# Where the first weight sums of the down projection stand in VectorE's order

## The chip, the cores and the metric

The kernel runs on one core of a Trainium2 chip. The metric is the device time of one execution in microseconds (us); for a set of runs it is their median. TensorE multiplies matrices, VectorE and ScalarE work on tiles, GpSimd does little here, and SyncE (SP) issues nearly all DMAs. Each engine works through its own instructions in one fixed order.

## The reference

A decoder trunk of two layers on 512 tokens of width 1024, in float32. Each layer is a half-step feed-forward block, a mixing block (three kinds of attention, gated and merged) and a second half-step feed-forward block. So there are four feed-forward blocks, named a0, c0, a1 and c1 here in their order in time. What matters is one of them:

```
def _swiglu(t, w_gate, w_up, w_down):
    return (jax.nn.silu(t @ w_gate) * (t @ w_up)) @ w_down

f = _swiglu(_rmsnorm(h, ffn1_pre_g[l]), ffn1_w_gate[l], ffn1_w_up[l], ffn1_w_down[l])
h = h + 0.5 * _rmsnorm(f, ffn1_post_g[l])
```

The hidden width is 2816, which is 22 tiles of 128.

## The kernel before

**Split operands.** A float32 product is made of three matmuls of a narrower format (mm3, lines 203 to 207): high times high, high times low, low times high. So each weight tile is split (lines 179 to 192): ScalarE casts the raw weight to its high part (wh, line 182), then VectorE subtracts that from the raw weight to get the low part (wl, line 183). Four buffers hold high parts and four hold low parts. A factor that comes from the hidden rows is split in the same way (ah, al).

**Seven products for eight.** Of the 22 hidden tiles, 16 are worked in two chunks of 8 (ci = 0, 1). In each chunk the hidden activations and the down weights are cut into 2 by 2 blocks, and the block product is made with seven products in place of eight, n = 0 to 6. Some products need sums of blocks. Line 282 says which weight block a product fetches; for n = 2 the sum is block (0, 1) minus block (0, 0). Block (0, 1) goes into a tile of its own that is kept for later products (bt, called bta and btc in the profile for the blocks a and c), block (0, 0) into a raw tile (raw_da, raw_dc), and line 327 subtracts one from the other on VectorE. Then the kept tile is split like any weight. Each product has two weight units of 128 x 1024 elements per tile, at k0 = 0 and k0 = 2; I call them a and b, and write (ci, n) for a product. The six hidden tiles that are left (f = 16 to 21) are worked plainly, and the gate and up products of the tiles 18 to 21 are put between the products of the down group.

**Order of the work.** products (lines 888 to 900) makes the down group's jobs in the order (0, 0), (1, 0), (0, 1), (1, 1), (0, 2), (1, 2), and so on (line 849). PLAN (lines 1643 to 1649) puts single jobs of the plain tiles between them. Around the change the order of the jobs is: (1, 0); gate of tile 18; (0, 1); (1, 1); gate of tile 19; (0, 2); up of tile 18; (1, 2); up of tile 19; (0, 3).

A queue (lines 350 to 461) works the jobs off. As a job begins, step calls load for its own weight units and then load_ahead, which loads the units of the following jobs until four units are counted. load (lines 318 to 331) fetches the unit if that has not been done, makes the sum where the product needs one, and splits. So the instructions of the loads are traced in this order:

- as the gate of tile 18 begins: the splits of (1, 1)a and (1, 1)b;
- as (0, 1) begins: sum and split of (0, 2)a, then sum and split of (0, 2)b;
- as (1, 1) begins: the splits of the up weights of tile 18, and behind them the factor of (0, 2) (first_factor, lines 829 to 847);
- as (0, 2) begins: sum and split of (1, 2)a, then of (1, 2)b.

**Order on the engine.** The order in which an engine gets its instructions is not the order of tracing. A scheduler sets it when the program is built, from priorities and from its own estimate of when each input is there. An instruction whose inputs it takes to be there early can thus go in front of others that were traced before it. tc.keep_in_program_order(ins) pins one instruction behind the one traced just before it on the same engine. That is an edge of order alone and adds no semaphore wait. In load the sum is pinned only while Q.pinned is set, which it is in one place (halved, lines 633 to 640, at the start of a block).

**Buffers and DMA.** Raw weights of the down group go into two rings: two buffers "raw" for the units a and two of the tag "o" for the units b. A raw buffer is free for the next transfer when its last reader is done; for (ci, 2) that is the sum, otherwise the low split. The up and gate weights of the plain tiles take "raw" buffers too. SyncE issues the transfers in its own fixed order.

Of the kernel before, what the change touches and what calls it, by code (L numbers as in the profile page):

```python
# [23 lines left out]
def kernel(  # L24
# [79 lines left out]
    def stile(shape, tag, name, dt=F32R):  # L104
        return sb.tile(shape, dt, tag=tag, bufs=BUFS[tag], name=name)
# [126 lines left out]
    class Unit:  # L232


        def __init__(self, src, k0, nk, c0, ncol, name, scale=None):
            self.tags, self.place = ("wh", "wl"), "raw"
            self.src, self.k0, self.nk, self.c0, self.ncol, self.name, self.scale = src, k0, nk, c0, ncol, name, scale
            self.h = self.raw = None
# [13 lines left out]
        def load(self):  # L252
            if self.h is not None:
                return
            self.fetch()
            self.split_from(self.raw[:])
            self.loaded()
# [16 lines left out]
    class BlockUnit(Unit):  # L274
# [9 lines left out]
        def __init__(self, n, src, rows, k0, nk, ncol, keep, name, place="raw"):  # L284
            super().__init__(src, k0, nk, 0, ncol, name)
            self.n, self.rows, self.keep, self.fetched, self.place = n, rows, keep, False, place
            self.heir = None

        def inherits(self, un):
            un.heir, self.place = self, None  # L290
# [27 lines left out]
        def load(self):  # L318
            if self.h is not None:
                return  # L320
            self.fetch()
            src = raw = self.raw[:]
            if self.n in (2, 3, 5, 6):
                t = self.keep.get(self.k0)
                src = raw if self.n == 5 else t
                a, b = (t, raw) if self.n in (2, 5) else (raw, t)
                ins = nc.vector.tensor_tensor(src, a, b, ALU.subtract)
                if Q.pinned:
                    tc.keep_in_program_order(ins)
            self.split_from(src)  # L330
            self.loaded()
# [131 lines left out]
    Q = Queue()  # L463
# [139 lines left out]
    def ffn(l, src, wg, wu, wd, dst, name, spare, parked, plan, aside=None):  # L603
# [247 lines left out]
        def product(at, uns):  # L851
            ci, n = DOWN[at]
            first, last = ci == 0, ci == NC - 1
            if at == 0:
                RINGS["o"] = 2
                dst.begin()
            if at + 1 < len(DOWN):
                first_factor(*DOWN[at + 1])
            if first and n in (0, 2):
                st["b", SUM[n]] = [pbank("z", f"pd{name}_{n}_{e}") for e in range(2)]  # L860
            pts = st["b", SUM[n]]
            h, l = st.pop(("a", ci, n))
            opens, ends = first and n in (0, 2), last and n in (1, 4, 6)
            for un in uns:
                for e in range(2):
                    c = slice(e * P, (e + 1) * P)
                    for k in range(un.nk):
                        kk = un.k0 + k
                        mm3(pts[e][:], h[:, kk, c], l[:, kk, c], un.h[:, k], un.l[:, k], opens and kk == 0,
                            ends and kk == FC // 2 - 1, free=True)  # L870
                        yield 3 * S * PE_US
                    turn(un.k0 + e)
            if not last:
                return
            if n == 0:
                st["b", 1] = [pbank("z", f"pd{name}_1_{e}") for e in range(2)]
                for e in range(2):
                    nc.scalar.copy(st["b", 1][e][:], pts[e][:])
                return
            i, hf = TO[n]  # L880
            for e in range(2):
                f = dst.fs[2 * i + e][:, HF[hf]]
                if n in (4, 5):
                    nc.vector.tensor_tensor(f, f, pts[e][:], ALU.add)
                else:
                    nc.scalar.copy(f, pts[e][:])

        def products():

            keep = [Keep(lambda k0, ci=ci: stile([P, 2, S], "o", f"bt{name}_{ci}_{k0}", F32)[:]) for ci in range(NC)]  # L890
            had = {}
            for at, (ci, n) in enumerate(DOWN):
                w = wd[l, ci * FC * P:(ci + 1) * FC * P]
                uns = [BlockUnit(n, w, FC // 2, k, 2, S, keep[ci], f"d{name}_{ci}_{n}_{k}", ("raw", "o")[k // 2])
                       for k in range(0, FC // 2, 2)]
                if n == 4:
                    for un, of in zip(uns, had[ci, 3]):
                        un.inherits(of)
                had[ci, n] = uns
                yield uns, (lambda at=at, uns=uns: product(at, uns))  # L900
# [18 lines left out]
        def queue(what):  # L919
            kind, n = what[0], what[1]  # L920
            if kind in "gu":
                if n not in made:
                    made[n] = plain(n)
                ms = (what[2],) if what[-1] in (0, 1) and len(what) == 3 else range(2)
                uns = made[n][kind == "u"]
                run = (lambda: gates(n, uns, ms)) if kind == "g" else (lambda: ups(n, uns, ms))
                Q.add(uns if ms[0] == 0 else [], run)
            elif kind == "a":
                Q.add([], lambda: iter(first_factor(n, 0) or ()))
            elif kind == "m":  # L930
                if name == "a0":
                    Q.add([], mem_stats)
            else:
                if what not in made:
                    made[what] = products() if kind == "d" else token_products(n, kind == "U")
                for one in made[what]:
                    Q.add(*one)
                    break
# [766 lines left out]
```

## Time and profile before

| | |
|---|---|
| median of three runs | 2383.31 us (2377.81 to 2385.16) |
| the profiled execution | 2377.93 us |
| its span, first to last instruction | 2376.2 us |
| mean granted clock of TensorE | 0.996 of full speed |
| VectorE busy | 1800.1 us, 76% of the span |
| ScalarE busy | 1511.8 us, 64% of the span |
| weight sums of product 2 in the down group (line 327) | 8 in blocks a, 1224 ns each, and 8 in blocks c, 1226 ns each (median) |

A timeline row of the profile gives the start and the length in us, the engine, the line of the kernel, the operation, the tile that is written and those that are read, and the shape. In brackets stand the idle time of the engine before it and what ended that time: "<-DMA raw_da" is a transfer into raw_da, "<-PE pda L207" a matmul of line 207 into pda. PE is TensorE, DVE is VectorE, ACT is ScalarE, SPq is SyncE's queue, where a row is the issue of a transfer and not the transfer. Buffers have no numbers, so two rows with the same tile names may be different units. In a list of waits a row reads: who waited, for whom, us in total, how often, the longest. PEclk is the clock that TensorE was granted, as a share of full speed.

### The profile page before, as it was taken

Reading aid. Unit: us, or ns where it says so; the run is one execution under the profiler, and the core shown is the slowest. Engines: PE = TensorE matmul, PEld = TensorE weight load, DVE = VectorE, ACT = ScalarE, POOL = GpSimd, SP = SyncE. Lnnn points to the kernel's source line nnn. Section 1 sums busy time; section 2 is a strip of 40 time slices with the busy share of each in tenths; the row PEclk is TensorE's granted clock in tenths of the full one; section 3 lists DMA queues with packets and bytes.
Section 4 is the critical chain, followed back from the end, with each engine's and each line's share of the span. In section 5 each row is a group of like instructions: output and inputs, shape, how many; then the busy total and the mean of one; then the engine's idle time right before and its main releaser. Section 6 shows DMA issues by size and latency. Waiting matters only on the chain.

```text
span 2376.2 us, 31130 instructions
## 1 busy us (share of the span) xinstructions
PE 2347.3 (99%) x11719; PEld 1986.0 (84%) x11719; DVE 1800.1 (76%) x2358; ACT 1511.8 (64%) x2305; POOL 75.4 (3%) x134
## 2 busy tenths in 40 slices
PE   9999999999999999999999999999999999999998
PEld 7787889888888888878888878899888888888787
DVE  8876877677777688868788768766767777887785
ACT  6776465576766556774556765646777665567744
POOL 0000000000111000000000000000000100000000
PEclk9999999999999999999999999999999999999999
DMA  5666454223323555664646664542323235566743
GB/s 204 185 177 199 154 190 142 80 83 88 89 74 104 192 189 160 186 186 146 226 127 198 205 171 147 194 129 72 94 76 98 72 117 188 174 185 175 214 144 142
DMA packets 299754, 354.98 MB, mean 149 GB/s; under 512 B 78266, under 2 KB 192978, under 8 KB 299604
## 3 DMA queue, kind: packets, MB, share of 16 engines
q1 hardware_dynamic: 299508, 352.97, 48.5%
q8 instruction: 92, 1.51, 0.3%
q14 instruction: 58, 0.48, 0.1%
q0 software_dynamic: 96, 0.03, 0.0%
HBM read 319.39 MB, written 16.78 MB: 141 GB/s over the span
## 4 chain that ended last, share of the span: by engine, by line
PE 89%; DMA 3%; DVE 3%; ACT 2%; issue 1%; SPq 0%; POOL 0%; DVEq 0%; ACTq 0%
PE pg L206 4%; PE pg L207 4%; PE pg L205 4%; PE pda L206 3%; PE pdc L206 3%; PE pda L207 3%; PE pda L205 3%; PE pdc L207 2%; PE pdc L205 2%; PE pb L206 2%; PE pb L207 2%; PE pb L205 2%; PE pwo L206 1%; PE pq L206 1%; PE pq L205 1%
## 5 line engine op out<-in xcount | busy, mean ns | idle before, releaser
L205 PE MATMUL pg<-us_a,wh_wg 128*128 128x512 f32 x384 | 151.0, 393 | 0.0
L206 PE MATMUL pg<-us_a,wh_wg 128*128 128x512 f32 x384 | 149.8, 390 | 0.0
L207 PE MATMUL pg<-us_a,wl_wg 128*128 128x512 f32 x384 | 149.8, 390 | 0.0
L206 PE MATMUL pda<-wl_da,aha 128*128 128x512 f32 x224 | 89.0, 398 | 6.6 <-DVE wl_da L183 6.6
L206 PE MATMUL pdc<-wl_dc,ahc 128*128 128x512 f32 x224 | 88.7, 396 | 6.1 <-DVE wl_dc L183 6.1
L183 DVE TENSOR_TENSOR wl_da<-raw_da,wh_da 128x1024 fp32r<-128x1024 f32 x50 | 60.8, 1223 | 37.4 <-ACT wh_da L182 37.3
L205 PE MATMUL pda<-wh_da,aha 128*128 128x512 f32 x224 | 88.2, 397 | 0.8 <-ACT wh_da L182 0.5
L207 PE MATMUL pda<-wh_da,ala 128*128 128x512 f32 x224 | 88.4, 395 | 0.0
L183 DVE TENSOR_TENSOR wl_dc<-raw_dc,wh_dc 128x1024 fp32r<-128x1024 f32 x50 | 60.9, 1222 | 35.8 <-ACT wh_dc L182 35.8
L207 PE MATMUL pdc<-wh_dc,alc 128*128 128x512 f32 x224 | 87.9, 393 | 0.0
L205 PE MATMUL pdc<-wh_dc,ahc 128*128 128x512 f32 x224 | 87.4, 393 | 0.4 <-ACT wh_dc L182 0.4
L207 PEld LDWEIGHTS pg<-us_a,wl_wg 128*128 128x128 f32 x384 | 72.1, 188 | 15.2
L205 PEld LDWEIGHTS pg<-us_a,wh_wg 128*128 128x128 f32 x384 | 72.1, 188 | 14.1
L206 PEld LDWEIGHTS pg<-us_a,wh_wg 128*128 128x128 f32 x384 | 72.2, 188 | 14.1
L182 ACT CAST wh_da<-raw_da 128x1024 fp32r<-128x1024 f32 x50 | 52.1, 1049 | 41.1 <-PE pda L207 11.1
L186 DVE SCALAR_TENSOR_TENSOR wl_wg<-raw_wg,wh_wg 128x1024 fp32r<-128x1024 f32 x48 | 58.4, 1221 | 23.0 <-ACT wh_wg L185 23.0
L182 ACT CAST wh_dc<-raw_dc 128x1024 fp32r<-128x1024 f32 x50 | 52.1, 1047 | 35.3 <-DMA raw_dc<-in_ffn_w_down_dram 11.5
L200 DVE SCALAR_TENSOR_TENSOR ga<-pg,bgate,ga 128x512 f32<-128x512 f32 x48 | 35.9, 747 | 48.7 <-ACT ga L199 48.7
L182 ACT CAST wh_uc<-raw_uc 128x1024 fp32r<-128x1024 f32 x44 | 46.4, 1054 | 37.6 <-PE pwc0g L207 8.6
L185 ACT ACTIVATE wh_wg<-raw_wg 128x1024 fp32r<-128x1024 f32 x48 | 50.5, 1057 | 25.5 <-PE pv L1096 11.7
L183 DVE TENSOR_TENSOR wl_uc<-raw_uc,wh_uc 128x1024 fp32r<-128x1024 f32 x44 | 53.7, 1220 | 16.7 <-ACT wh_uc L182 16.6
L182 ACT CAST wh_ua<-raw_ua 128x1024 fp32r<-128x1024 f32 x44 | 46.2, 1052 | 28.7 <-PE pga L206 7.2
(647 smaller groups left out, 8057.2 us busy)
## 6 DMA issues: line engine op xcount, KB each, us to landing
raw_da<-in_ffn_w_down_dram SPq DMA_DIRECT2D x66, 512.0 KB, 4.9
raw_dc<-in_ffn_w_down_dram SPq DMA_DIRECT2D x66, 512.0 KB, 3.8
raw_ga<-in_ffn_w_gate_dram SPq DMA_DIRECT2D x52, 512.0 KB, 4.7
raw_ua<-in_ffn_w_up_dram SPq DMA_DIRECT2D x52, 512.0 KB, 4.6
raw_gc<-in_ffn_w_gate_dram SPq DMA_DIRECT2D x52, 512.0 KB, 4.1
raw_uc<-in_ffn_w_up_dram SPq DMA_DIRECT2D x52, 512.0 KB, 4.2
raw_wg<-in_w_gate_dram SPq DMA_DIRECT2D x48, 512.0 KB, 3.5
raw_wo<-in_w_out_dram SPq DMA_DIRECT2D x24, 512.0 KB, 3.6
```

Of the source, the lines that this page charges most:

```text
L182: both = [nc.scalar.copy(h_ap, src)]
L183: make = lambda: nc.vector.tensor_tensor(l_ap, src, h_ap.bitcast(F32), ALU.subtract)
L185: both = [nc.scalar.activation(h_ap, src, AF.Copy, scale=scale)]
L186: make = lambda: nc.vector.scalar_tensor_tensor(l_ap, src, scale, h_ap.bitcast(F32), ALU.mult, ALU.subtract)
L200: nc.vector.scalar_tensor_tensor(t, z, minus, t, ALU.max, ALU.add)
L205: nc.tensor.matmul(pt, lh, rh, start=start, stop=False, skip_group_check=free)
L206: nc.tensor.matmul(pt, lh, rl, start=False, stop=False, skip_group_check=free)
L207: nc.tensor.matmul(pt, ll, rh, start=False, stop=stop, skip_group_check=free)
```

## The change

A weight unit gets a mark, behind. products sets it on the units of product 2, in both chunks and in all four feed-forward blocks. Where it is set, load pins the sum of line 327 behind the instruction traced just before it on VectorE, as Q.pinned does. Sums of the other products, and those of the gate and up groups (token_products), stay as they were.

```diff
@@ BlockUnit.__init__
-            self.heir = None
+            self.heir, self.behind = None, False
@@ BlockUnit.load
                 ins = nc.vector.tensor_tensor(src, a, b, ALU.subtract)
-                if Q.pinned:
+                if Q.pinned or self.behind:
                     tc.keep_in_program_order(ins)
@@ products
                 uns = [BlockUnit(n, w, FC // 2, k, 2, S, keep[ci], f"d{name}_{ci}_{n}_{k}", ("raw", "o")[k // 2])
                        for k in range(0, FC // 2, 2)]
+                for un in uns:
+                    un.behind = n == 2
                 if n == 4:
```

## The prediction

> **What bounds the kernel now.** I read the page first, then the waits of TensorE alone, then the timelines of VectorE, ScalarE, TensorE and the DMA queue around the longest of those waits, and last a table by stretch for the clock.
>
> ```profile
> span 2376.2 us, 31130 instructions
> ...
> PE 2347.3 (99%) x11719; PEld 1986.0 (84%) x11719; DVE 1800.1 (76%) x2358; ACT 1511.8 (64%) x2305; POOL 75.4 (3%) x134
> ```
>
> TensorE is busy in all but 28.9 us of its span. A change of order on VectorE can therefore pay in two ways only: it takes away part of those 28.9 us, or it takes away matmuls that run slowly. The waits of TensorE say who owns the idle time:
>
> ```profile
> PE pda L206 <- DVE wl_da L183: 6.6, 2, 4.3
> PE pdc L206 <- DVE wl_dc L183: 6.1, 2, 4.4
> ```
>
> Four waits, 12.7 us, all of the down group (pda, pdc) and all for the low part of a weight (wl). One lies in each of the four feed-forward blocks. I write (ci, n) for product n of chunk ci, and a and b for its two weight units. In the first block VectorE's timeline reads:
>
> ```profile
> 213.49 1.23 DVE L327 TENSOR_TENSOR bta<-bta,raw_da 128x1024 f32<-128x1024 f32 x1 [2.38 <-DMA raw_da<-in_ffn_w_down_dram]
> 216.17 1.22 DVE L327 TENSOR_TENSOR bta<-bta,raw_da 128x1024 f32<-128x1024 f32 x1 [1.46 <-DMA raw_da<-in_ffn_w_down_dram]
> 217.32 1.22 DVE L183 TENSOR_TENSOR wl_da<-raw_da,wh_da 128x1024 fp32r<-128x1024 f32 x1
> 218.45 1.22 DVE L183 TENSOR_TENSOR ala<-asa,aha 128x1024 fp32r<-128x1024 f32 x1
> 219.59 1.22 DVE L838 TENSOR_TENSOR asa<-hra,hra 128x1024 f32<-128x1024 f32 x1
> 220.72 1.22 DVE L183 TENSOR_TENSOR wl_da<-raw_da,wh_da 128x1024 fp32r<-128x1024 f32 x1
> ```
>
> The first two rows are the weight sums of (0, 2), units a and b. Both sit waiting for their DMA. Behind them, with no idle time of their own, come the low parts of (1, 1)a at 217.32 and (1, 1)b at 220.72, a product that runs *earlier*. ScalarE and TensorE beside it:
>
> ```profile
> 214.12 1.04 ACT L182 CAST wh_da<-raw_da 128x1024 fp32r<-128x1024 f32 x1
> 216.09 1.04 ACT L182 CAST wh_da<-raw_da 128x1024 fp32r<-128x1024 f32 x1 [0.93 <-PE pda L207]
> 222.50 1.04 ACT L182 CAST wh_da<-bta 128x1024 fp32r<-128x1024 f32 x1 [5.37 <-PE pda L207]
> ```
>
> ```profile
> 215.89 0.39 PE L205 MATMUL pda<-wh_da,aha 128*128 128x512 f32 x1
> 218.59 0.50 PE L206 MATMUL pda<-wl_da,aha 128*128 128x512 f32 x1 [2.31 <-DVE wl_da L183]
> ```
>
> The high part of (1, 1)a was cast from 214.12, done at 215.16, and TensorE took it up at 215.89. Only the low part was missing, and it stood behind the sum of 216.17, which waited for a transfer. That is what ends last in this stage.
>
> The waits cost more than themselves, because the clock drops behind them:
>
> ```profile
> 220.01:223.42 3.41, 3.41 (x10) 0.50 0.82 292
> 1056.28:1063.10 6.82, 4.32 (x10) 0.50 0.56 187
> 1397.61:1404.43 6.82, 4.32 (x10) 0.50 0.71 210
> 2236.18:2237.86 1.68, 0.00 (x1) 1.00 0.59 208
> ```
>
> After each stretch and its length stand TensorE's busy time with its instructions, its granted clock, and the share and rate of the DMA. Behind the waits of 2.31, 4.41 and 4.27 us the clock is 0.50 for 3.41, 4.32 and 4.32 us of busy time; half of that is lost: 1.71 + 2.16 + 2.16 = 6.03 us. The wait of 1.68 us keeps its clock.
>
> **The change part by part.** It adds no instruction, byte or semaphore wait; it adds 16 edges of order on VectorE (4 blocks, 2 chunks, 2 units).
>
> (0, 2)a, four times. The instruction traced in front is the low split of (1, 1)b, since the jobs load in this order. Its sum moves behind 220.72. This is the edge that acts.
>
> (0, 2)b, four times. In front of it stands the low split of (0, 2)a. It moves even further back, out of the way as well.
>
> (1, 2)a and (1, 2)b, eight edges. In front stand the low part of the factor of (0, 2), at 218.45, and the low split of (1, 2)a:
>
> ```profile
> 235.38 1.23 DVE L327 TENSOR_TENSOR bta<-bta,raw_da 128x1024 f32<-128x1024 f32 x1 [2.10 <-DMA raw_da<-in_ffn_w_down_dram]
> 237.80 1.22 DVE L183 TENSOR_TENSOR wl_da<-bta,wh_da 128x1024 fp32r<-128x1024 f32 x1 [1.19 <-ACT wh_da L182]
> 238.94 1.22 DVE L327 TENSOR_TENSOR bta<-bta,raw_da 128x1024 f32<-128x1024 f32 x1
> ```
>
> Both sums are already behind (235.38 after 218.45, 238.94 after 237.80), so these edges cost and give nothing.
>
> What is late next, once the two sums are out of the way? The low split of (1, 1)a needs the cast. A split that waits for its cast starts 1.08 us after the cast's start (222.50 above, 223.58 here):
>
> ```profile
> 223.58 1.23 DVE L183 TENSOR_TENSOR wl_da<-bta,wh_da 128x1024 fp32r<-128x1024 f32 x1 [0.50 <-ACT wh_da L182]
> ```
>
> and the matmul follows 1.27 us after the split's start (217.32 to 218.59). So the matmul comes 2.35 us after the start of the cast. In the first block 214.12 + 2.35 = 216.47 in place of 218.59: 2.12 us gained. Nothing else ready on VectorE holds it up: the split at 218.45 and the sum at 219.59 can go into the idle 2.38 us in front of 213.49 or wait. The other blocks, cast and waiting matmul of each:
>
> ```profile
> 1052.78 1.98 ACT L182 CAST wh_dc<-raw_dc 128x1024 fp32r<-128x1024 f32 x2
> ```
>
> ```profile
> 1058.78 0.79 PE L206 MATMUL pdc<-wl_dc,ahc 128*128 128x512 f32 x1 [4.41 <-DVE wl_dc L183]
> ```
>
> ```profile
> 1394.25 1.98 ACT L182 CAST wh_da<-raw_da 128x1024 fp32r<-128x1024 f32 x2
> ```
>
> ```profile
> 1400.11 0.79 PE L206 MATMUL pda<-wl_da,aha 128*128 128x512 f32 x1 [4.27 <-DVE wl_da L183]
> ```
>
> ```profile
> 2234.61 1.03 ACT L182 CAST wh_dc<-raw_dc 128x1024 fp32r<-128x1024 f32 x1
> ```
>
> ```profile
> 2237.86 0.50 PE L206 MATMUL pdc<-wl_dc,ahc 128*128 128x512 f32 x1 [1.68 <-DVE wl_dc L183]
> ```
>
> Second block: 1052.78 + 2.35 = 1055.13, 3.65 us gained. Third: 1396.60, 3.51 us. Fourth: 2236.96, 0.90 us. Together 2.12 + 3.65 + 3.51 + 0.90 = 10.18 us. What is left of each wait is 0.2 to 0.8 us, below the 1.68 us that kept its clock, so the 6.03 us of half clock go too. The sum is 16.2 us; at most, with the waits gone altogether, 12.7 + 6.0 = 18.7 us.
>
> Here a rule of the Trainium skill can be weighed (page "TensorE: Matmul & The Clock Gate", section "Why this matters for your kernels"): it asks for no TensorE gap over about 3 us to keep the clock up. The wait of 2.31 us in the first block is shorter and the half clock follows it all the same, so the trace speaks against that figure here. By the rule the 1.7 us of the first block would have another cause and stay, and the sum would be 14.5 us.
>
> The moved sums free buffers, and that is where a cost could come from:
>
> ```profile
> 214.74 4.19 SPq L249 DMA_DIRECT2D raw_ua<-in_ffn_w_up_dram  x2
> 218.98 0.50 SPq L297 DMA_DIRECT2D bta<-in_ffn_w_down_dram  x1
> 231.50 0.37 SPq L297 DMA_DIRECT2D raw_da<-in_ffn_w_down_dram  x1
> ```
>
> ```profile
> raw_ua<-in_ffn_w_up_dram SPq DMA_DIRECT2D x52, 512.0 KB, 4.6
> ```
>
> The first of the two raw_ua transfers (the next up weights) goes out at 214.74, as the sum of 213.49 ends; the second goes out when the split of 217.32 ends. With the change the sum runs after the split of (1, 1)b: cast 216.09 + 1.08 = 217.17, then 1.14 us on (the spacing of VectorE's rows, 217.32 to 218.45) the sum from 218.31 to 219.53. The transfer then lands at 219.53 + 4.6 = 224.1. It is used here:
>
> ```profile
> 228.25 1.06 ACT L182 CAST wh_ua<-raw_ua 128x1024 fp32r<-128x1024 f32 x1
> ```
>
> ```profile
> 230.26 1.22 DVE L183 TENSOR_TENSOR wl_ua<-raw_ua,wh_ua 128x1024 fp32r<-128x1024 f32 x1
> ```
>
> The cast moves up with TensorE by 2.12 + 1.71 = 3.83 us, to 224.42. The transfer is in time by 0.3 us in this block; the other three, worked out in the same way, leave more. Behind the split of 230.26 hangs the issue of 231.50, and behind that (1, 2):
>
> ```profile
> 242.35 1.21 DVE L183 TENSOR_TENSOR wl_da<-bta,wh_da 128x1024 fp32r<-128x1024 f32 x1
> ```
>
> ```profile
> 241.65 0.39 PE L207 MATMUL pua<-us_x,wl_ua 128*128 128x512 f32 x1
> 241.88 0.39 PE L205 MATMUL pda<-wh_da,aha 128*128 128x512 f32 x1
> ```
>
> TensorE starts a matmul every 0.23 us and reaches unit b after 12 of them, at 244.6; its low part is done at 243.56. So there is 1.0 us of cover. If the transfer came later than that, every further microsecond would be one of waiting. I cost it at nothing, with 0 to 2 us for each block as its bounds.
>
> **The rivals.**
>
> *Part of the gain.* The half clock has another cause than the waits, or other instructions of VectorE (the split of 218.45, the sum of 219.59) take the place in front of (1, 1)a. Then some 10 us stay as gain: 2373 us. For it: the scheduler lays all that follows anew, and the half clock of the first block begins 1.4 us after the wait has ended. Against: each of the three waits over 2 us has its half clock beside it, and the one below has none.
>
> *No change.* The edge doesn't bind where it counts, or a wait of the same size shows up next (the split waits for a cast that moves as well): 2383 us. Against: the cast is 1 to 4 us ahead of the split in every block.
>
> *Slower.* The wait moves to (1, 2). The mechanism: the buffer of the next up weights comes free with the *second* sum, which is now behind the split of (0, 2)a and so behind a cast that waits for TensorE; the transfer, the split of 230.26 and the transfers of (1, 2) all come later. The price is at most that of the largest wait seen, 4.41 us and 2.16 us of half clock, in four blocks: 26.3 - 16.2 = 10.1 us slower, 2393 us. It decides from the point at which the up weights come more than 1.0 + 4.4 us after their cast could run, issued after 225 us in the first block. Against: the second sum would end at about 223, which makes this a wait of 2 us rather than 4.
>
> **How the numbers follow.** The profiled execution took 2377.93 us, 1.7 us beyond its span; 16.2 us less is 2361.7 us. The median of the three runs, 2383.31 us, lies 5.4 us above the profiled one, and the same work off it gives **2367.1 us**, which I forecast. Chances: forecast (gain of 12 to 19 us) 0.64, part of the gain 0.16, no change 0.11, slower 0.09. About 0.3%, 7 us, is what a measurement of this kernel can tell from no change. Faster by more: 0.64 + 0.16 = 0.80; within: 0.11; slower by more: 0.09. The low end is the fastest run less 18.7 us, 2359, with 1 us to spare: 2358. The high end takes in the partial gain with up to 2 us lost per block and leaves out most of no change and slower: 2380.
>
> **What would show it.** Right: in each block the low splits of (1, 1)a and b stand ahead of both L327 sums of (0, 2) on VectorE; TensorE's waits for wl_da and wl_dc fall from 12.7 to under 3 us; no stretch of clock 0.50 is left but the first and last; TensorE's busy time falls by about 6 us and its idle time by about 10. Wrong: new waits of TensorE at pda or pdc one or two products later; raw_ua or raw_uc landing after ScalarE has come to their cast; clock 0.50 behind waits under 1 us; the same four waits behind another instruction of VectorE.

## The result, and the profile after

| | before | after |
|---|---|---|
| median, us | 2381.1 (4 runs, 2377.81 to 2385.16) | 2364.81 (4 runs, 2362.99 to 2365.65) |
| the profiled execution, us | 2377.93 | 2364.23 |
| its span, us | 2376.2 | 2362.5 |

The ratio is 0.9928, with a 95% interval from 0.9914 to 0.9943: the kernel is faster by 0.7%, 16.3 us between the medians and 13.7 us between the two profiled executions. The forecast was 2367.1 us in a range of 2358 to 2380.

The head of the page of after:

```profile
span 2362.5 us, 31122 instructions
...
PE 2341.4 (99%) x11719; PEld 1980.5 (84%) x11719; DVE 1798.8 (76%) x2358; ACT 1510.6 (64%) x2305; POOL 75.4 (3%) x134
```

TensorE's busy time fell by 5.9 us (2347.3 to 2341.4), its idle time by 7.8 us (28.9 to 21.1). Both parts of the forecast gain are there, but not in these sizes: in the first 15 us, ahead of every edge, the busy time is 1.7 us shorter and the idle time 1.2 us longer than in before. The table of stretches below leaves that out. The longest waits of TensorE in after:

```profile
PE utc L578 <- DVE nhc L484: 1.5, 1, 1.5
PE utx L1597 <- DVE fx L1606: 1.3, 2, 0.9
PE warm L1567 <- DVE warm L1659: 1.3, 1, 1.3
PE pwa0g L205 <- ACT pwa0g L747: 1.3, 1, 1.3
PE pdc L206 <- DVE wl_dc L183: 1.2, 2, 0.8
PE pwa0g L207 <- DVE ula L183: 1.1, 1, 1.1
PE pda L206 <- DVE wl_da L183: 0.8, 1, 0.8
PE pwo L206 <- DVE wl_wo L183: 0.7, 1, 0.7
```

The two rows that had 6.6 and 6.1 us have 0.8 and 1.2. VectorE in the first block of after:

```profile
215.28 1.23 DVE L183 TENSOR_TENSOR wl_da<-raw_da,wh_da 128x1024 fp32r<-128x1024 f32 x1 [4.13 <-ACT wh_da L182]
216.42 1.22 DVE L183 TENSOR_TENSOR ala<-asa,aha 128x1024 fp32r<-128x1024 f32 x1
217.55 1.22 DVE L838 TENSOR_TENSOR asa<-hra,hra 128x1024 f32<-128x1024 f32 x1
218.69 1.22 DVE L183 TENSOR_TENSOR wl_da<-raw_da,wh_da 128x1024 fp32r<-128x1024 f32 x1
219.82 1.22 DVE L327 TENSOR_TENSOR bta<-bta,raw_da 128x1024 f32<-128x1024 f32 x1
220.96 1.22 DVE L840 TENSOR_TENSOR asa<-asa,hra 128x1024 f32<-128x1024 f32 x1
222.24 1.22 DVE L183 TENSOR_TENSOR wl_da<-bta,wh_da 128x1024 fp32r<-128x1024 f32 x1
223.38 1.22 DVE L327 TENSOR_TENSOR bta<-bta,raw_da 128x1024 f32<-128x1024 f32 x1
```

Read it from the top: the low split of (1, 1)a waits for its cast and for nothing else, then come the splits that are ready, (1, 1)b at 218.69, and only then the sums of (0, 2) at 219.82 and 223.38. Neither of the two sums waits for its transfer any more, since it has landed by then. The other three blocks have the same order. In the same stage the cast on ScalarE, the matmul that had waited 2.31 us, and the matmuls that had waited 4.41, 4.27 and 1.68 us:

```profile
214.19 1.05 ACT L182 CAST wh_da<-raw_da 128x1024 fp32r<-128x1024 f32 x1
```

```profile
216.04 0.39 PE L205 MATMUL pda<-wh_da,aha 128*128 128x512 f32 x1
216.56 0.50 PE L206 MATMUL pda<-wl_da,aha 128*128 128x512 f32 x1
```

```profile
1052.58 0.50 PE L206 MATMUL pdc<-wl_dc,ahc 128*128 128x512 f32 x1 [0.76 <-DVE wl_dc L183]
```

```profile
1389.13 0.50 PE L206 MATMUL pda<-wl_da,aha 128*128 128x512 f32 x1 [0.76 <-DVE wl_da L183]
```

```profile
2224.16 0.50 PE L206 MATMUL pdc<-wl_dc,ahc 128*128 128x512 f32 x1 [0.42 <-DVE wl_dc L183]
```

In the first block 216.04 + 0.39 = 216.43, so TensorE is idle for 0.13 us, too little for a bracket of its own.

And the clock, by stretches of after (columns as in the prediction's table of stretches, with the weight loads, VectorE, ScalarE and GpSimd between):

```profile
220.20:223.60 3.40, 3.40 (x16) 2.75 (x16) 3.34 (x4) 2.45 (x4) 0.00 (x0) 1.00 0.36 70
1050.50:1057.30 6.80, 5.64 (x23) 3.83 (x22) 6.01 (x6) 1.84 (x3) 0.00 (x0) 1.00 0.53 170
1387.00:1393.80 6.80, 5.60 (x22) 3.79 (x22) 5.95 (x6) 1.84 (x3) 0.00 (x0) 1.00 0.51 163
```

The granted clock is 1.00 where it was 0.50. In all of after it is 0.50 only in the first 12 and the last 3 us.

**Where the 13.7 us came from.** By operation and tiles, TensorE works the same 11719 matmuls in the same order in both traces, so a new order of TensorE is no part of the gain, and the start of one can be subtracted from the start of the same one. In a block the first part of the gain is what the waiting matmul starts earlier, the second what is gained behind it, where before has the half clock:

| stretch, up to (us, by the times of before) | how far after is ahead, us: at its begin, at its end | gain | forecast |
|---|---|---|---|
| start to the first block's wait, 216 | 0, -0.15 | -0.15 | 0 |
| block a0, 226 | -0.15, 3.38 | 2.18 + 1.35 = 3.53 | 2.12 + 1.71 = 3.83 |
| to block c0, 1054 | 3.38, 2.55 | -0.83 | 0 |
| block c0, 1064 | 2.55, 8.01 | 3.66 + 1.80 = 5.46 | 3.65 + 2.16 = 5.81 |
| to block a1, 1395 | 8.01, 7.46 | -0.55 | 0 |
| block a1, 1406 | 7.46, 12.79 | 3.52 + 1.81 = 5.33 | 3.51 + 2.16 = 5.67 |
| to block c1, 2236 | 12.79, 12.41 | -0.38 | 0 |
| block c1, 2238 | 12.41, 13.70 | 1.29 | 0.90 |

The four places give 15.6 us against a forecast of 16.2: 10.65 us of waits against 10.18, and 4.96 us of clock against 6.03. The other 1.9 us are given back in between, at small waits that are longer than before: 1.3 us at 128.75 (pwa0g, 0.5 before), 0.7 us at 844 (pwo, no row of its own before) and 1.5 us at 1179.94 (utc, 1.1 before). The first of them lies ahead of every edge, and over the thirteen traces of this text it takes 0.3 to 1.5 us, so not all of this belongs to the change.

### The profile page after: what moved, and what is told of

Read it like the earlier page. It is cut to its first block, busy times and chain, and to the rows that moved or that the text cites. A ratio compares the mean times of both kernels' runs of the same rounds, so it can differ in the third digit from the quotient of the medians.

```text
span 2362.5 us, 31122 instructions
## 1 busy us (share of the span) xinstructions
PE 2341.4 (99%) x11719; PEld 1980.5 (84%) x11719; DVE 1798.8 (76%) x2358; ACT 1510.6 (64%) x2305; POOL 75.4 (3%) x134
## 4 chain that ended last, share of the span: by engine, by line
PE 85%; DVE 4%; DMA 4%; ACT 4%; issue 2%; SPq 0%; POOL 0%; DVEq 0%; ACTq 0%
PE pg L206 4%; PE pg L205 4%; PE pg L207 4%; PE pda L206 3%; PE pda L207 3%; PE pda L205 3%; PE pdc L206 2%; PE pdc L207 2%; PE pdc L205 2%; PE pb L206 2%; PE pb L207 2%; PE pb L205 2%; PE pq L206 1%; PE pq L205 1%; PE pk L207 1%
## 5 line engine op out<-in xcount | busy, mean ns | idle before, releaser
L182 ACT CAST wh_uc<-raw_uc 128x1024 fp32r<-128x1024 f32 x44 | 46.4, 1054 | 35.3 <-PE pwc0g L207 8.3
```

The costliest lines, as they stand in the source:

```text
L182: both = [nc.scalar.copy(h_ap, src)]
```

## The experiments

My theory: the gain is the low split of (1, 1)a standing in front of the sums that wait for their transfers. The rivals: it comes from other edges, or from the new order that the scheduler laid everywhere. Each kernel is the changed one with the edit shown. Kernels that were measured together share their runs of before; others are compared by their ratios to before.

**1. Which edges act.** Three kernels set the mark on a part of the sums only.

```diff
-                    un.behind = n == 2
+                    un.behind = (ci, n, un.k0) == (0, 2, 0)      # unit a of (0, 2) alone
+                    un.behind = (ci, n, un.k0) == (0, 2, 2)      # or unit b of (0, 2) alone
+                    un.behind = (ci, n) == (1, 2)                # or the second chunk alone
```

Unit a of (0, 2):

> Only the sum of (0, 2)a is pinned; the other 15 edges are taken out. My theory: one in-order queue, and whichever sum waits longest for its transfer sets the time. The sum of (0, 2)b stays ahead of the low split of (1, 1)a and waits for its transfer as before, so the four waits of TensorE stay at about 2.3, 4.4, 4.3 and 1.7 us with three half clocks behind them, and the time is that of the kernel before, within 4 us (0.2%). The rival, that the edge next to the split (unit a) is the one that acts, expects the whole gain, about 16 us, or most of it.

2381.77 us (10 runs) beside 2380.28 of before: ratio 1.0003 (0.9994 to 1.0013). The four waits stay, and VectorE shows why:

```profile
218.21 1.23 DVE L327 TENSOR_TENSOR bta<-bta,raw_da 128x1024 f32<-128x1024 f32 x1 [6.23 <-DMA raw_da<-in_ffn_w_down_dram]
219.35 1.22 DVE L183 TENSOR_TENSOR wl_da<-raw_da,wh_da 128x1024 fp32r<-128x1024 f32 x1
```

```profile
PE pdc L206 <- DVE wl_dc L183: 7.3, 2, 4.3
PE pda L206 <- DVE wl_da L183: 7.1, 2, 4.0
```

The sum of unit a is out of the way (it comes at 223.89), that of unit b still stands in front of the split and waits for its transfer.

Unit b of (0, 2):

> Only the sum of (0, 2)b is pinned. My theory: the sum of (0, 2)a stays ahead of the low split of (1, 1)a, but its transfer lands about when that split's cast is done, so it delays the split by 0 to 1.1 us a block; the sum of b, which waited until 216.2 in the first block, is gone. Waits of TensorE at wl_da and wl_dc of 0.1 to 1.9 us each, at most one half clock; 12 to 16 us faster than before, 0 to 4 us slower than the whole change. The rival that unit a acts expects no gain here.

2365.25 us (4 runs), ratio 0.9935 (0.992 to 0.9949). Here the sum of unit a is ahead, and harmless:

```profile
213.14 1.23 DVE L327 TENSOR_TENSOR bta<-bta,raw_da 128x1024 f32<-128x1024 f32 x1 [1.58 <-DMA raw_da<-in_ffn_w_down_dram]
215.66 1.23 DVE L183 TENSOR_TENSOR wl_da<-raw_da,wh_da 128x1024 fp32r<-128x1024 f32 x1 [1.29 <-ACT wh_da L182]
```

It is done at 214.37, before the split could start anyway: the split goes on waiting, now for the cast. Only in the second block does unit a still cost much, a wait of 2.1 us where the change has 0.8:

```profile
PE pdc L206 <- DVE wl_dc L183: 2.5, 2, 2.1
```

The second chunk:

> Only the two sums of (1, 2) are pinned. My theory: they stand behind their neighbours anyway, so nothing changes: the time before within 4 us, the four waits and three half clocks as before. The rival, that the gain comes from everything behind being laid anew, expects a part of the gain.

2380.72 us (10 runs), ratio 1.0003 (0.9993 to 1.0012). The waits of TensorE are as long as before or longer:

```profile
PE pda L206 <- DVE wl_da L183: 8.7, 2, 4.7
PE pdc L206 <- DVE wl_dc L183: 6.4, 2, 4.2
```

The eight edges of (1, 2) give nothing.

**2. More edges.** The mark on all sums that have one:

```diff
-                    un.behind = n == 2
+                    un.behind = n in (2, 3, 5, 6)
```

> All sums of the down group are pinned (products 2, 3, 5 and 6). No wait of TensorE over 0.5 us is left behind a sum in the down group after the change, so there is nothing to win: within 3 us of the changed kernel, and slower by 2 to 8 us if a pinned sum comes so late that its cast runs out of cover (1.0 us at (1, 2)b). The rival, that sums in front of splits cost everywhere, expects 2 to 4 us more of gain.

2369.08 us (4 runs), ratio 0.995 (0.9935 to 0.9965): some 4 us of the gain are lost, though the interval overlaps that of the change (0.9914 to 0.9943) a little. The largest part is one new wait of TensorE, in the mixing block, for an instruction of VectorE, and that one waits for a transfer:

```profile
327.75 0.44 PE L1051 MATMUL mt<-ident,mraw 128*128 128x128 f32 x2 [2.15 <-DVE mraw L1044]
326.94 0.75 DVE L1044 TENSOR_SCALAR mraw<-mraw,mem_rstd 128x1024 f32<-128x1024 f32 x1 [1.52 <-DMA mraw<-in_mem_dram]
```

The expectation had a late sum at (1, 2)b as the way to lose time; this is another one. No pinned sum stands in front of mraw. Its transfers go out from 320.15 on, in the change from 316.32 on. How the edges moved them was not followed up.

**3. The split made late without any sum.** Behind the low split of (1, 1)a VectorE works the half of it again, two, three or four times; the matmul waits for the last of them. A half repeat takes 0.6 us.

```diff
@@ BlockUnit.load
             self.split_from(src)
+            for k in range(self.again):
+                tc.keep_in_program_order(nc.vector.tensor_tensor(
+                    self.l[:, k % 2], src[:, k % 2], self.h[:, k % 2].bitcast(F32), ALU.subtract))
@@ products
-                    un.behind = n == 2
+                    un.behind, un.again = n == 2, 2 * ((ci, n, un.k0) == (1, 1, 0))      # or 3 *, or 4 *
```

Twice:

> The changed kernel, with the low split of (1, 1)a followed by two repeats of half its columns each (128x512) that TensorE has to wait for. A repeat takes about 0.60 us of VectorE, so the split is 1.2 us late; the result is the same. My theory: waits of TensorE one for one, about 1.3, 2.0, 2.0 and 1.6 us in the four blocks in place of 0.1, 0.8, 0.8 and 0.4, 4.8 us in all; a half clock behind the two of 2.0 is open (none at 1.68, one at 2.31 so far), 0 to 3.4 us more. So 5 to 8 us slower than the changed kernel. By the page's 3 us: 5 us, no half clock.

Three times:

> Three repeats, 1.8 us late. Waits of about 1.9, 2.6, 2.6 and 2.2 us, 7.2 us in all. My theory: a half clock of 3.4 us (1.7 us lost) behind the two of 2.6, perhaps behind the others: 10.6 to 14 us slower than the changed kernel. By the page's 3 us no half clock at all: 7.2 us slower.

Four times:

> Four repeats, 2.4 us late. Waits of about 2.5, 3.2, 3.2 and 2.8 us, 9.6 us in all, and a half clock behind each, 1.7 to 2.2 us: 16 to 18 us slower than the changed kernel, so the time of the kernel before without any sum in the way. By the page's 3 us a half clock behind two alone: 13 to 14 us. If the gain had come from elsewhere than these waits, the time would stay below that of before by most of 16 us.

Measured, with before at 2379.73 us: 2368.8 us (ratio 0.9952, 0.9938 to 0.9967), 2366.41 us (0.9945, 0.993 to 0.996) and 2367.17 us (0.9947, 0.9927 to 0.9968). All three lie 1.6 to 5.7 us above the change, by medians or by ratios, and the time does not grow with the repeats. The last two expectations were wrong, and by the last sentence of the third this outcome would speak for a gain from elsewhere. But the waits that were to be made did not come: in the last kernel they are 0.33, 1.30, 1.28 and 1.14 us, with no half clock between the first 15 us and the end. Its rows tell why. VectorE does what it should, TensorE does not:

```profile
214.65 1.23 DVE L183 TENSOR_TENSOR wl_da<-raw_da,wh_da 128x1024 fp32r<-128x1024 f32 x1 [4.24 <-ACT wh_da L182]
215.91 2.50 DVE L332 TENSOR_TENSOR wl_da<-raw_da,wh_da 128x512 fp32r<-128x512 f32 x4
```

```profile
216.24 0.39 PE L205 MATMUL pga<-us_x,wh_ga 128*128 128x512 f32 x1
...
217.15 0.39 PE L206 MATMUL pga<-us_x,wh_ga 128*128 128x512 f32 x1
217.86 0.50 PE L206 MATMUL pda<-wl_da,aha 128*128 128x512 f32 x1 [0.33 <-DVE wl_da L332]
```

The scheduler, which knows of the added work on VectorE as the program is built, has put five matmuls of the next gate job (pga) in front of the one that waits. Of 2.5 us of delay 0.33 are left as a wait. In the kernel before, the same matmuls stood behind the waiting one.

**4. The same, with TensorE's order held.** So the jobs (1, 1) and gate of tile 19 were pinned on TensorE in the order of tracing, with no repeat, two and four (the repeats as above).

```diff
+    def held(gen):
+        with in_order(nc.tensor):
+            yield from gen
@@ the jobs of products and of the gates
-                yield uns, (lambda at=at, uns=uns: product(at, uns))
+                yield uns, (lambda at=at, uns=uns: held(product(at, uns)) if DOWN[at] == (1, 1) else product(at, uns))
-                run = (lambda: gates(n, uns, ms)) if kind == "g" else (lambda: ups(n, uns, ms))
+                run = (lambda: held(gates(n, uns, ms)) if (n, ms) == (18, (1,)) else gates(n, uns, ms)) if kind == "g" else (lambda: ups(n, uns, ms))
```

> The change, with TensorE's order of the jobs (1, 1) and gate of tile 19 held as traced in each block, and nothing delayed. My theory (the gain is the low splits of (1, 1) standing ahead of the sums): same as the change, 2363 to 2367 us, four waits of at most 1.3 us at the low part of (1, 1). A rival by which the scheduler's new order of TensorE, and not VectorE's, makes the gain: some of it goes, 2370 us or more.

> As the held order, and two more half splits (about 1.2 us of VectorE) behind the low split of (1, 1)a, so that it is late by that much and TensorE can't fill the time with matmuls of the next gate job. My theory: waits of about 1.3, 2.0, 2.0 and 1.6 us at the low part of (1, 1), 4.8 us in all over the change, and a half clock (1.7 us each) only where 1.7 us of idle time or more falls into one window of 3.41 us, none to two of them: 5 to 8 us slower than the change. Rival (the gain came from elsewhere, the place of the low split is nothing to the time): 2364 to 2368 us.

> As the run with two, with four half splits (about 2.4 us). My theory: waits of about 2.5, 3.2, 3.2 and 2.8 us, 9.6 us over the change, and up to four half clocks of 1.7 us: 12 to 17 us slower than the change, near the time of the kernel before, without a sum ahead of the split. Rival (the gain came from elsewhere): 2364 to 2368 us.

| held order, repeats | median, us | ratio to before (95%) | waits at the low part of (1, 1), a0, c0, a1, c1, us |
|---|---|---|---|
| none | 2362.73 (4 runs) | 0.9914 (0.9891 to 0.9936) | 0.14, 0.76, 0.75, 0.30 |
| two | 2368.44 (4 runs) | 0.9937 (0.9917 to 0.9957) | 0.58, 1.48, 1.48, 0.71 |
| four | 2374.04 (8 runs) | 0.9966 (0.9954 to 0.9979) | 2.13, 2.69, 2.68, 1.90 |

before had 2382.15 us in these runs. The time now rises by 5.7 and by 11.3 us with the delay, and no sum is in front of the split in any of the three. Held order alone costs nothing. With four repeats the matmul that waited 4.41 us in the second block of before waits again, on another cause:

```profile
1055.12 0.50 PE L206 MATMUL pdc<-wl_dc,ahc 128*128 128x512 f32 x1 [2.69 <-DVE wl_dc L332]
```

The sizes came out small. Counted from the change itself, as the expectations have it, the two kernels are 3.6 and 9.2 us slower, where 5 to 8 and 12 to 17 were expected; counted from the held order, 5.7 and 11.3. The waits of the run with four are 0.4 to 0.9 us shorter than expected. The rival (2364 to 2368 us) is excluded by the run with four: seven of its eight executions took 2373.56 us or more. The profiled one, 2367.76 us, is the exception. Its four waits are 7.5 us longer than those of the held order, and it has a half clock in the second block, but it is only 3.9 us slower than that one's profiled execution. The two traces have the same order of matmuls and show where most of the rest went: 2.0 us come back right behind the waits, mainly where the held order waits for the low part of (1, 1)b (0.37 to 0.41 us a block) and this run does not, and 1.3 us at the wait for utc, which it does not have either.

**5. How much cover (1, 2) has.** Four half repeats behind the low split of (0, 2)a put off all that follows on VectorE by 2.5 us.

```diff
-                    un.behind = n == 2
+                    un.behind, un.again = n == 2, 4 * ((ci, n, un.k0) == (0, 2, 0))
```

> The changed kernel, with four half repeats behind the low split of (0, 2)a, so that the sum of (0, 2)b and all that follows on VectorE is 2.4 us later. My theory (the mechanism of the rival slower): there is 1.0 us of cover at (1, 2)b, and from there on a microsecond costs a microsecond: waits of TensorE of about 1.4 us at the low split of (1, 2)b in each block, 5.6 us slower than the changed kernel, no half clock. If the transfers have more cover, no change; if they have none, 9.6 us.

2367.73 us (4 runs), ratio 0.9953 (0.9938 to 0.9968): 3 to 6 us above the change. The first block:

```profile
242.27 1.22 DVE L183 TENSOR_TENSOR wl_da<-bta,wh_da 128x1024 fp32r<-128x1024 f32 x1
```

```profile
239.33 0.39 PE L205 MATMUL pda<-wh_da,aha 128*128 128x512 f32 x1
...
242.50 0.39 PE L205 MATMUL pua<-us_x,wh_ua 128*128 128x512 f32 x1
242.73 0.39 PE L206 MATMUL pua<-us_x,wh_ua 128*128 128x512 f32 x1
243.55 0.50 PE L206 MATMUL pda<-wl_da,aha 128*128 128x512 f32 x1 [0.43 <-DVE wl_da L183]
```

(1, 2) starts at 239.33 and would need the low part of unit b 13 matmuls of 0.23 us later, at 242.3. It gets it at 243.55, so 2.5 us of delay make 1.25 us of lateness: the cover is about 1.2 us. The prediction had 1.0 us, with 12 matmuls counted for 13. Of the lateness 0.43 us show as a wait here, since two matmuls of the up job and one more of (1, 2) were put in front. The four blocks together wait 2.1 us, less than the 5.6 expected.

## Why the prediction was right, and where not

**The bound.** Right. Four waits with the half clock behind three of them were what this change could reach, and they are what went. (For the fourth, the prediction shows the clock of the wait itself; in the 3.4 us behind it, from 2237.86, it is 1.00 too.)

**Which edge acts.** Wrong. The prediction says of (0, 2)a "This is the edge that acts" and lets (0, 2)b only go "out of the way as well". The mark on unit a alone gives nothing; the mark on unit b alone keeps nearly the whole gain. The step that failed is the choice of the sum that the split waits for last, and the rows of before had it: the sum of unit a, 213.49, was done at 214.72, before the cast of (1, 1)a ended at 215.16. The sum of unit b, 216.17, was the last that the split waited for. The sum of the terms did not suffer, since both edges were in the change. Unit a is worth about 1.3 us in the second block (wait 2.1 us with it ahead, 0.8 without). The edges of (1, 2) do nothing, as worked out.

**What is late next.** Right, nearly to the hundredth: the matmul comes 2.35 us after the start of the cast. 214.19 to 216.56 is 2.37 us; the remaining waits are 0.13, 0.76, 0.76 and 0.42 us where 0.2 to 0.8 were worked out.

**The half clock.** Right in kind, too large in size, and tested. With the waits it went, and with the delay of four repeats it came back in one block without any sum in the way. Behind the three waits it gave 1.35, 1.80 and 1.81 us where 1.71, 2.16 and 2.16 were counted. Half of the busy time was too much: at the half clock of before a matmul starts every 0.43 us (1059.38, 1059.80, 1060.23) and not every 0.46, which is twice 0.23, and after itself loses 0.1 to 0.2 us at the next low part. That TensorE's busy time fell by 5.9 us, nearly the 6.03, is luck: 1.7 us of it lie in the first 15 us. The stretches of the kernel with the held order and four repeats:

```profile
1053.27:1056.68 3.41, 1.56 (x7) 1.28 (x8) 3.41 (x5) 0.00 (x0) 0.00 (x0) 1.00 0.02 8
1056.68:1060.09 3.41, 3.41 (x10) 2.67 (x9) 3.41 (x4) 1.04 (x1) 0.00 (x0) 0.50 0.85 192
```

TensorE is idle for 3.41 - 1.56 = 1.85 us of the first stretch, and the next has the clock 0.50. The reading that a wait is what counts, with a bound between 1.68 and 2.31 us, was too simple: see the last section.

**The sums of the terms.** 15.6 us of 16.2 in the four places. The first three blocks gave 0.3 us less each than worked out, all of it at the clock, and the fourth 0.4 us more, at the wait. What I costed at nothing, the rest of the program, cost 1.9 us. Whether the new schedule or the single execution makes these waits is open. Waits like the one at 844 us come to 0.2 to 1.1 us in all in the other kernels that have them.

**The moved sum and the up weights.** The sum of (0, 2)a ends at 221.04, not at 219.53: between the two splits the scheduler put the low part of the factor (216.42) and line 838 (217.55), which I had let go first or wait. That was no harm. The transfers of the up weights and their second cast in after:

```profile
216.53 4.91 SPq L249 DMA_DIRECT2D raw_ua<-in_ffn_w_up_dram  x2
```

```profile
227.59 1.06 ACT L182 CAST wh_ua<-raw_ua 128x1024 fp32r<-128x1024 f32 x1 [0.90 <-PE pga L206]
```

The last of the two goes out by 221.44, and the cast waits for TensorE and not for the transfer. At (1, 2) no wait is left in the first block.

**The rivals.** *Part of the gain*: the split of 218.45 did get in between, but behind (1, 1)a, and the half clock went with the waits. *No change*: this is what the edges on unit a or on (1, 2) alone do. *Slower*: the condition was an issue after 225 us; it was 221.4. The last link of its mechanism is real, as the fifth experiment shows (about 1.2 us of cover, then a wait at (1, 2)); late transfers of the up weights themselves were not tried. With 2.5 us of delay the four waits there come to 2.1 us, because part of the lateness is filled with other matmuls, and the whole kernel lost 3 to 6 us, far from the 6.6 us per block that the rival had as its most.

**The time.** 2364.81 against 2367.1 us. The profiled execution should have taken 2361.7 us and took 2364.23: 2.5 us less gain, the 1.9 us that were given back and the 0.6 in the four places. The median fell by more, 16.3 us, since the profiled execution of before was a short one, 3.2 us under the median of its four runs, and that of after is 0.6 us under its own. So the forecast came out 2.3 us high although the gain of the profiled execution was less than worked out. That the medians differ by just about the 16.2 us of the sum is luck.

## What to carry to other kernels

Where a ready instruction stands in an in-order queue behind several that wait for transfers, look for the one that ends last: here it carried nearly all of the wait, and the edge on it alone nearly all of the gain. Put an edge where the trace shows a wait, not on every instruction of the kind: here the other edges gave nothing or cost some 4 us. Work that is added on one engine lets the scheduler move other work into the wait that it makes; to price a wait by adding work, hold the order of the engine that waits.

## What the runs showed of the hardware

**The clock goes by windows, not by waits.** In every trace here the stretches of half clock that lie behind the first 15 us and before TensorE's last matmul are 3.41 us long or twice that, and the stretches between them whole multiples of 3.413 us (836.265 us is 245 of them). So I counted TensorE's idle time in each window of that length, again without the first 15 us and without the windows from TensorE's last matmul on. Over the thirteen traces 22 windows have 1.68 us or more idle; behind 20 of them the clock is 0.50, behind two it is not (1.78 and 1.81 us). No window that has the full clock and 1.63 us idle or less is followed by it; one that has the half clock itself and 0.99 us idle is (second chunk alone, 220.88 to 224.29 us). The bound is not sharp: in three traces the window in which TensorE's last matmul ends has 1.72, 1.80 and 1.93 us idle and is followed by the full clock, and in the first 15 us the half clock follows windows with 0.6 to 1.5 us idle. Waits of 0.43 and 1.25 us within one window bring the half clock (two repeats, order not held, second block); a wait of 2.05 us that falls into two windows with 0.74 and 1.31 us does not (unit b alone, second block). Two windows of the kernel with the held order and two repeats, each with the next one:

```profile
1051.15:1054.56 3.41, 1.72 (x6) 1.05 (x6) 2.97 (x4) 1.32 (x2) 0.00 (x0) 1.00 0.30 109
1054.56:1057.97 3.41, 3.41 (x9) 2.64 (x8) 3.41 (x4) 0.08 (x1) 0.00 (x0) 0.50 0.54 154
1180.85:1184.26 3.41, 1.78 (x12) 1.66 (x13) 3.34 (x7) 1.80 (x6) 0.00 (x0) 1.00 0.40 109
1184.26:1187.67 3.41, 3.41 (x21) 2.90 (x20) 3.32 (x8) 2.06 (x6) 0.00 (x0) 1.00 0.82 246
```

1.69 us idle and the half clock follows; 1.63 us idle, in one wait that is longer than any in the first, and it does not. The Trainium skill (page "TensorE: Matmul & The Clock Gate", Part 1, "What's actually happening") has a free-running window of 3413 ns, which the trace agrees with, and a drop after at least one idle window; here about half a window of idle time is enough in 20 of those 22 windows.

**A wait of this size has no fixed price.** In the kernel with the held order and four repeats the wait of 2.69 us in the second block has the half clock behind it, and the wait of 2.68 us in the third has not. Where the windows lie differs from one execution to the next: in all thirteen traces the first matmul starts 1.3 us into the span, and the first edge of a window lies anywhere from 0.3 to 3.3 us into it. This kernel took 2367.76 us in its profiled execution, with one half-clock window inside, and 2373.56 to 2376.35 us in the seven others, at a lower mean clock (0.996 to 0.998 against 0.999). That the windows cut the same waits in another way there would explain up to 8.6 us of difference, but it is not shown, since only one execution was traced.
